# Weight buffers moved by 64 bytes, and thirteen products 32 columns wider, in a two-layer transformer step

## The chip, the cores and the metric

The kernel runs on one core of a Trainium2 chip. Its time is that of the whole program in device microseconds, the median of several runs. A profiled execution gives the trace from which all views here are taken.

Engines: TensorE (PE; its weight loads are listed as PEld), VectorE (DVE), ScalarE (ACT), GpSimd (POOL), SyncE (SP), and 16 DMA engines. SBUF is the on-chip memory of 128 partitions; an address below is a byte offset within a partition.

## What is computed

One step of a model with two layers, for 128 context tokens and 128 latent tokens, all in float32. Each layer is a mixer (attention) and a feed-forward; the change touches the feed-forward of the first layer alone:

```python
def conv_ffn(h, w_up, w_conv, b_conv, w_down):
    u = h @ w_up                                   # (128, 2048) x (2048, 11264), for both groups
    up = jnp.pad(u, ((0, 0), (1, 1), (0, 0)))
    u = up[:, :-2] * w_conv[0] + up[:, 1:-1] * w_conv[1] + up[:, 2:] * w_conv[2] + b_conv
    gate, val = u[..., :D_FF], u[..., D_FF:]       # D_FF = 5632
    return (jax.nn.silu(gate) * val) @ w_down
```

Around it stand a normalisation with a learned shift and scale before, and a gate and a residual sum behind it. The shifts, scales and gates come from a large product of the condition with `w_ada`.

## The kernel before

Both groups of tokens are kept together as 256 columns, features on the partitions. A product of float32 accuracy is made of three in the type float32r: each operand is split into a high and a low part, and `gemm` (line 382) issues, for each block of 128 features, high weights by high activations, high weights by low ones, and low weights by high ones. Each is one weight load of 128x128 and one product with 256 moved columns, all from the one line 111. A chunk is one output block of 128 features: 16 blocks, so 48 products, in the up-projection; 22 blocks, so 66 products, in the down-projection. The activations are `hx` (up) and `g` (down), high and low halves of 256 columns side by side in one row of 512.

The feed-forward (`ffn`, line 1527) goes in two halves: 44 up chunks (gate and value chunks in turn, each followed by the convolution `cv`), 16 down chunks, and the same again. So there are four parts: up, down, up, down.

Weights come through the class `Weights` (line 254). SP issues a DMA of 1 MB into `raw` (three buffers). The first 8 blocks are copied by ACT into `wh` (high part, line 249), and DVE subtracts to make `wl` (line 250), four buffers each, used in turn by the second 8 blocks too. In the first feed-forward two tiles in five take another way for their second 8 blocks (`go_far`, `prepare`, lines 287 to 302): ACT copies into `farh` (line 299), ACT writes its negative into `farl` (line 300), and POOL issues a DMA (line 301) that reads the weights from memory once more and adds them into `farl`, so that DVE needn't. There are two buffers of each, 43 far half-tiles of 24 products in all, 30 of them in up chunks. Nothing else in the program uses `farh` and `farl`.

Beside this, DVE works off the `w_ada` sums (line 499, tile `araw`) between its other work, at rates fixed by the table `FRATE`.

The tile framework fixes the order of instructions on each engine when the program is built, and places every buffer. The places that matter here, by the built program, in bytes:

| tile | role | first byte | remainder by 128 |
|---|---|---|---|
| `hx` | moved operand, up | 27,264 | 0 |
| `g` | moved operand, down | 151,168 (22 tiles, the others from 153,216 on) | 0 |
| `wh`, `wl` | weights | 104,128 and 120,512 (first of four each) | 64 |
| `farh`, `farl` | weights | 212,608 and 220,800 (first of two each) | 0 |

All blocks in these tiles are multiples of 512 bytes apart, so that the remainder is the same for all of them.

Products of more columns than needed are in the kernel already: the first products of five up chunks of each feed-forward move more than 256 columns (`WIDER`, 32, 16, 8, 4 and 2 more, through `more` in `gemm`). The surplus columns of the result are never read. In the second mixer, the list `PUSH` does the like.

Of the kernel before, what the change touches and what calls it, by code (L numbers as in the profile page):

```python
# [18 lines left out]
P = 128  # L19
# [3 lines left out]
NT = 2 * T  # L23
# [30 lines left out]
RATE = {"in0": 0.35, "in": 0.5, "in3": 0.25, "heads": 0.72, "out0": 0.62, "c": 0.36, "outc": 0.36}  # L54
FRATE = [{"up": 0.9, "down": 1.8}, {"up": 0.7, "down": 1.42}]
LEAD = (9, 3)
PEW = {"heads": 1.0, "out0": 1.0, "c": 1.0}
QUIET = [4, 3, 3]
LATE = 3
# [2 lines left out]
WIDER = (32, 16, 8, 4, 2)  # L62
# [33 lines left out]
def step_kernel(ctx: ExitStack, tc: tile.TileContext, A: dict):  # L96
# [36 lines left out]
    def banks(name):  # L133
        return tc.tile_pool(name=name, bufs=1, space=PSUM)
# [3 lines left out]
    def nm(s):  # L138
        uid[0] += 1
        return f"{s}_{uid[0]}"  # L140

    def T_(pl, shape, tag, dt=F32, bufs=None):
        kw = {} if bufs is None else {"bufs": bufs}
        return pl.tile(shape, dt, tag=tag, name=nm(tag), **kw)
# [11 lines left out]
    def C(name):  # L156
        a, w = _AT[name]
        return cst[:, a:a + w]
# [89 lines left out]
    def split(out_hi, out_lo, src, pin=lambda i: i):  # L248
        pin(act.copy(out_hi, src))  # L249
        pin(dve.tensor_tensor(out=out_lo, in0=src, in1=out_hi.bitcast(F32), op=ALU.subtract))  # L250

    fine = [False]

    class Weights:

# [35 lines left out]
        def prepare(self):  # L291
            while len(self.begun) < 2 and self.at < self.until:
                self.begun.append(self.load())
            for raw, n in self.begun:
                i = next(i for r, i in self.index if r is raw)
                if i in self.span and i % 5 in (1, 3) and not any(m[0] is raw for m in self.made):
                    wh = T_(self.far, [P, 1024], "farh", F32R, bufs=2)
                    wl = T_(self.far, [P, 1024], "farl", F32R, bufs=2)
                    act.copy(wh, raw[:, 8 * P:n * P])
                    act.activation(wl, wh.bitcast(F32), AF.Copy, scale=-1.0)  # L300
                    pool.dma_start(out=wl, in_=self.src[i, :, 8 * P:n * P], accum_op=ALU.add)
                    self.made.append((raw, wh, wl))
# [182 lines left out]
    def load_row():  # L485
        feat["row"] = T_(feat["home"], [P, 2, D], "condb")
        sp.dma_start(out=feat["row"], in_=A["condb"])
        for r in range(2):
            keep_order(act.activation(feat["row"][:, r], feat["row"][:, r], AF.Silu))
# [30 lines left out]
    class Deep:  # L520
# [44 lines left out]
        def pump(self):  # L565
            self.due += self.rate
            while self.due >= 1.0:
                self.due -= 1.0
                if self.steps:
                    self.step()  # L570
# [82 lines left out]
    def ensure(l, j, qs=range(4)):  # L653
        for u in [(l, j, q) for q in qs]:
            while u in ROWS and u not in done and ada["i"] <= ROWS.index(u):
                row_step()
            while u in FEATS and u not in done:
                feature_step()
            while u in DEEP[l] and u not in done:
                deep.step()  # L660
            while u not in done:
                later.pop(0)()
# [95 lines left out]
    def raw_tile(pl, tag):  # L758
        return home(pl, tag)[:, :KD * 2 * UW].rearrange("p (k n) -> p k n", k=KD)
# [183 lines left out]
    def mixer_ab(hx, beside):  # L943
        l = 0
        with tc.tile_pool(name="ab", bufs=1) as ab:
# [297 lines left out]
            with tc.tile_pool(name="abh", bufs=1) as hp:  # L1243
                ada["pew"] = PEW["heads"]

# [91 lines left out]
    def out_ab(o, st, u, beside, rp):  # L1337
        l = 0
        rows = raw_rows(u, l, 1)
        ensure(l, 2)  # L1340
        ada["pew"] = PEW["out0"]
        W = Weights(A["w_out_ab"], KD, 1)
# [184 lines left out]
    def ffn(hx, W, ready, turn, l, st):  # L1527
        xh, xl = (lambda k: hx[:, k, :NT]), (lambda k: hx[:, k, NT:2 * NT])
        wider = list(WIDER)
        long = len(ready) > 3  # L1530

        def product():
            if ready:
                return ready.pop(0)
            if in_order:
                return gemm(W.chunk(), xh, xl, between=in_order.pop(0))
            if wider:
                n = NT + wider.pop(0)
                return gemm(W.chunk(), xh, xl, more=lambda k: hx[:, k, :n])
            return gemm(W.chunk(), xh, xl)  # L1540

        WD = Weights(A["w_down"][l], KQ, TB)
        cw = ada["cw"]
        with tc.tile_pool(name=f"ffn{l}", bufs=1) as fp, banks(f"pffn{l}") as pf:
            feat["home"], feat["pool"] = fp, pf
            feat["due"] = 0.0
            in_order = [{}, {}] + turn + [{}]
            T_(fp, [P, SHIFT // 4], "pad")

            def conv(m):  # L1550
                early = bool(ready)
                pin = keep_order if early else lambda i: i
                if len(ready) > 4 - 2 * long:
                    W.ahead(pin)
                ps = product()
                y = T_(fp, [P, NT], "cv", bufs=3)
                pin(act.activation(y, ps, AF.Identity, scale=cw[:, 1, m:m + 1], bias=cw[:, 3, m:m + 1]))  # L1557
                y3 = y.rearrange("p (g t) -> p g t", g=2)
                p3 = ps.rearrange("p (g t) -> p g t", g=2)
                pin(dve.scalar_tensor_tensor(out=y3[:, :, 1:], in0=p3[:, :, :T - 1],  # L1560
                                             scalar=cw[:, 0, m:m + 1], in1=y3[:, :, 1:],
                                             op0=ALU.mult, op1=ALU.add))
                pin(dve.scalar_tensor_tensor(out=y3[:, :, :T - 1], in0=p3[:, :, 1:],  # L1563
                                             scalar=cw[:, 2, m:m + 1], in1=y3[:, :, :T - 1],
                                             op0=ALU.mult, op1=ALU.add))
                if early and ready and not long:
                    W.ahead(pin)
                return y

            def up(q):  # L1570
                gs = []
                for i in range(q * KQ, (q + 1) * KQ):
                    rate = 0 if i < LATE else FRATE[l]["up"]
                    fine[0] = False
                    gate = conv(i)
                    pump(0, rate)
                    val = conv(NFF + i)
                    pump(0, rate)
                    act.activation(gate, gate, AF.Silu)
                    dve.tensor_tensor(out=val, in0=gate, in1=val, op=ALU.mult)  # L1580
                    g = T_(fp, [P, ROW], "g", F32R, bufs=KQ)
                    split(g[:, :NT], g[:, NT:2 * NT], val)
                    gs.append(g)
                    if i == LATE - 1:
                        load_row()
                return gs

            def down(gs, q):
                u, rows = None, None
                if q == NQ - 1 and l < NL - 1:  # L1590
                    u = raw_tile(keep, "hx")
                    rows = raw_rows(u, l + 1, 0)
                for c in range(KD):
                    quiet = q == NQ - 1 and c >= KD - QUIET[0]
                    fine[0] = quiet
                    if q == 0:
                        ensure(l, 5, [c // 4])
                    ps = gemm(WD.chunk(), lambda k: gs[k][:, :NT], lambda k: gs[k][:, NT:2 * NT])
                    if l == NL - 1 and q == NQ - 1 and c == KD - 1:
                        last_residual(ps, l, 1, c, st)  # L1600
                    else:
                        residual(ps, l, 1, c, st if q == NQ - 1 else None)
                    if rows:
                        rows(c)
                    if l == NL - 1 and q == NQ - 1 and c in EARLY:
                        act.activation(x[:, c], x[:, c], AF.Identity, scale=C("gfin")[:, c:c + 1])
                    pump(0, 0 if quiet else FRATE[l]["down"])
                return u

            for q in range(NQ):  # L1610
                if l == 0:
                    at, n = 2 * KQ * q, KQ * KD // TB
                    W.go_far(fp, at + LEAD[q], at + 2 * KQ, at + 2 * KQ)
                    WD.go_far(fp, n * q + 3, n * q + n, n * q + n - 6 * q)
                gs = up(q)
                u = down(gs, q)
            while feat["i"] < FLIMIT[stage[0]]:
                feature_step()
            return u
# [26 lines left out]
    with tc.tile_pool(name="cc", bufs=1) as cp, banks("pc") as ppool["ada"]:  # L1646
# [6 lines left out]
        st = stat_init()  # L1653
        ada["pew"] = PEW["c"]
        u = mixer_c(cp, hx, W, begun[0], st)
# [155 lines left out]
```

## Time and profile before

| what | value |
|---|---|
| median of 3 runs | 2322.39 us (2319.88 to 2324.16) |
| profiled execution | 2326.57 us, span 2324.8 us |
| mean granted TensorE clock | 0.993 |
| first feed-forward, first chunk with a wider product to last down product | 481.07 to 1193.22 us |
| second feed-forward, the same | 1632.28 to some 2312 us |
| DMA | 639.68 MB, mean 275 GB/s |

The page gives busy shares by engine and the chain of work that ended last. The windows view counts instructions in stretches of the span: since TensorE never rests, a stretch's length divided by its count of products is the time from one product to the next. The timeline lists instructions with their starts; equal neighbours are merged into one row with a count, and brackets tell what an engine waited for.

### The profile page before, as it was taken

To read this page: it belongs to the slowest core of one execution; us is meant where nothing else is said; L and a number is where in the kernel's file an instruction comes from. 1 tells how busy PE (TensorE), PEld (TensorE's weight loads), DVE (VectorE), ACT (ScalarE), POOL (GpSimd) and SP (SyncE) were. 2 spreads that over 40 slices of the span, in tenths; PEclk is the share of its full clock that TensorE was granted. 3 is DMA by queue.
4 is the path that set the end of the run, shared out by engine and by line. 5 is a ranking of instruction groups with operands and counts; after the bars stand their busy time and mean duration, and the time that the engine had idled before them with its cause. 6 is when DMAs were issued, how large, how long until landed. Compare 5 with 4: busy or idle time off the path is not lost.

```text
span 2324.8 us, 47335 instructions
## 1 busy us (share of the span) xinstructions
PE 2292.3 (99%) x19388; PEld 2209.0 (95%) x19388; DVE 1888.9 (81%) x2975; ACT 1231.6 (53%) x1999; POOL 227.8 (10%) x281
## 2 busy tenths in 40 slices
PE   8899999999999999999999999999999999999998
PEld 6788878999999999999999999999999999999998
DVE  4668979889888998989978989998999965666654
ACT  4346555675554455555565455557655434555543
POOL 0012111300000000000230000024000000000011
PEclk9999999999999999999999999999999999999999
DMA  9988879789889999998977887766767655555553
GB/s 380 366 335 307 327 287 366 290 296 305 293 301 318 350 318 305 304 311 291 325 262 268 338 277 272 257 217 214 253 259 269 257 200 198 188 195 200 188 194 127
DMA packets 106313, 639.68 MB, mean 275 GB/s; under 512 B 11440, under 2 KB 19568, under 8 KB 39536
## 3 DMA queue, kind: packets, MB, share of 16 engines
q1 hardware_dynamic: 99904, 614.11, 71.1%
q0 software_dynamic: 6192, 22.55, 5.3%
q8 instruction: 152, 2.49, 0.4%
q14 instruction: 65, 0.53, 0.1%
HBM read 631.86 MB, written 4.75 MB: 274 GB/s over the span
## 4 chain that ended last, share of the span: by engine, by line
PE 94%; DVE 2%; DMA 2%; POOL 1%; ACT 1%; issue 0%; SPq 0%; DVEq 0%; ACTq 0%; POOLq 0%
PE acc L111 89%; PE ada L111 3%; PE att L111 2%; DMA kvb<-w_ada 1%; DVE wl L250 1%; PE att L114 1%; DMA farl<-w_up 0%; PE misc L111 0%; DMA araw<-w_ada 0%; POOL dev L833 0%; DVE hx L551 0%; PE ada L114 0%; DVE x L1668 0%; POOL hxc L837 0%; ACT wh L249 0%
## 5 line engine op out<-in xcount | busy, mean ns | idle before, releaser
L111 PE MATMUL acc<-hx,wh 128*128 128x256 f32 (+1 forms) x6784 | 1188.8, 280 | 5.2 <-ACT wh L249 1.7
L249 ACT CAST wh<-raw 128x1024 fp32r<-128x1024 f32 (+2 forms) x791 | 749.7, 961 | 765.7 <-PE acc L111 637.4
L250 DVE TENSOR_TENSOR wl<-raw,wh 128x1024 fp32r<-128x1024 f32 (+2 forms) x791 | 876.3, 1121 | 264.6 <-ACT wh L249 260.8
L111 PEld LDWEIGHTS acc<-hx,wh 128*128 128x128 f32 x6784 | 1032.8, 189 | 24.0 <-issue 8.5
L111 PE MATMUL acc<-hx,wl 128*128 128x256 f32 (+1 forms) x3392 | 946.0, 279 | 4.7 <-DVE wl L250 4.4
L111 PEld LDWEIGHTS acc<-hx,wl 128*128 128x128 f32 x3392 | 639.5, 189 | 8.1 <-DVE wl L250 6.3
L111 PE MATMUL acc<-g,wh 128*128 128x256 f32 x2608 | 452.7, 279 | 0.0
L111 PEld LDWEIGHTS acc<-g,wh 128*128 128x128 f32 x2608 | 396.6, 189 | 0.0
L111 PE MATMUL acc<-g,wl 128*128 128x256 f32 x1304 | 362.5, 278 | 0.0
L499 DVE CUSTOM_DVE_ANT_0 junk<-araw,condb 128x2048 f32<-128x2048 f32 x152 | 349.5, 2299 | 1.3 <-DMA araw<-w_ada 1.3
L111 PEld LDWEIGHTS acc<-g,wl 128*128 128x128 f32 x1304 | 245.1, 188 | 0.0
L111 PE MATMUL acc<-hxc,wh 128*128 128x256 f32 (+1 forms) x1056 | 188.9, 281 | 0.0
L111 PEld LDWEIGHTS acc<-hxc,wh 128*128 128x128 f32 x1056 | 161.7, 188 | 1.0 <-issue 0.8
L212 POOL TENSOR_TENSOR sqacc<-sqacc,sq 128x256 f32<-128x256 f32 x62 | 73.1, 1178 | 878.6 <-ACT sq L208 878.4
L111 PE MATMUL acc<-hxc,wl 128*128 128x256 f32 (+1 forms) x528 | 146.8, 278 | 0.0
L1557 ACT ACTIVATE cv<-acc,convw 128x256 f32<-128x256 f32 x169 | 94.3, 558 | 19.9 <-PE acc L111 19.7
L111 PEld LDWEIGHTS acc<-hxc,wl 128*128 128x128 f32 x528 | 99.5, 189 | 0.2
L111 PE MATMUL acc<-wh,hxc 128*128 128x256 f32 (+1 forms) x512 | 94.3, 282 | 0.8 <-DVE nt L844 0.8
L111 PE MATMUL acc<-hx,farh 128*128 128x256 f32 x480 | 88.6, 285 | 0.0
L551 DVE CUSTOM_DVE_ANT_0 hx<-block,condb 128x1024 fp32r<-128x1024 f32 x65 | 79.4, 1222 | 6.8 <-DMA block<-w_ada 6.3
L1563 DVE SCALAR_TENSOR_TENSOR cv<-acc,convw,cv 128x254 f32<-128x254 f32 x169 | 81.1, 480 | 3.5
L1560 DVE SCALAR_TENSOR_TENSOR cv<-acc,convw,cv 128x254 f32<-128x254 f32 x169 | 80.5, 477 | 3.3 <-ACT cv L1557 3.3
(275 smaller groups left out, 2280.3 us busy)
## 6 DMA issues: line engine op xcount, KB each, us to landing
raw<-w_up SPq DMA_DIRECT2D x176, 1024.0 KB, 5.3
araw<-w_ada SPq DMA_DIRECT2D x136, 1024.0 KB, 6.9
raw<-w_down SPq DMA_DIRECT2D x88, 1024.0 KB, 5.0
raw<-w_in_c SPq DMA_DIRECT2D x48, 1024.0 KB, 6.6
block<-w_ada SPq DMA_DIRECT2D x41, 512.0 KB, 5.9
raw<-w_in_ab SPq DMA_DIRECT2D x18, 1024.0 KB, 9.2
raw<-w_out_ab SPq DMA_DIRECT2D x16, 1024.0 KB, 8.1
raw<-w_out_c SPq DMA_DIRECT2D x16, 1024.0 KB, 6.1
```

The costliest lines, as they stand in the source:

```text
L111: return self.placed(nc.tensor.matmul(*a, **kw))
L114: return self.placed(nc.tensor.transpose(*a, **kw))
L212: eng.tensor_tensor(out=st["acc"], in0=st["acc"], in1=sq, op=ALU.add)
L249: pin(act.copy(out_hi, src))
L250: pin(dve.tensor_tensor(out=out_lo, in0=src, in1=out_hi.bitcast(F32), op=ALU.subtract))
L499: keep_order(dve.tensor_tensor_reduce(out=T_(feat["pool"], [P, D], "junk"), in1=feat["row"][:, c], in0=feat["raw"].rearrange("p g n -> p ( ...
L551: keep_order(dve.tensor_tensor_reduce(out=self.junk, in0=self.raw, in1=self.row[:, c].rearrange("p (g n) -> p g n", g=2), scale=1.0, scala ...
L1557: pin(act.activation(y, ps, AF.Identity, scale=cw[:, 1, m:m + 1], bias=cw[:, 3, m:m + 1]))
L1560: pin(dve.scalar_tensor_tensor(out=y3[:, :, 1:], in0=p3[:, :, :T - 1], scalar=cw[:, 0, m:m + 1], in1=y3[:, :, 1:], op0=ALU.mult, op1=ALU.add))
L1563: pin(dve.scalar_tensor_tensor(out=y3[:, :, :T - 1], in0=p3[:, :, 1:], scalar=cw[:, 2, m:m + 1], in1=y3[:, :, :T - 1], op0=ALU.mult, op1=A ...
```

## The change

A pad of 16 floats (64 bytes) is allocated once, ahead of the first `farh`. It moves `farh` to 212,672 and `farl` to 220,864, so that both have the remainder 64 by 128. No other tile of the program moves. And in the first feed-forward (`l == 0`), of the up chunks counted from the first one that has a wider product, each sixth one gets a first product that moves 288 columns instead of 256. The first of those, chunk 6, comes after the five of `WIDER`.

```diff
+FARPAD = 16
+BEAT = 6
...
     fine = [False]
+    pads = []
...
                 if i in self.span and i % 5 in (1, 3) and not any(m[0] is raw for m in self.made):
+                    if not pads:
+                        pads.append(T_(self.far, [P, FARPAD], "farpad"))
                     wh = T_(self.far, [P, 1024], "farh", F32R, bufs=2)
                     wl = T_(self.far, [P, 1024], "farl", F32R, bufs=2)
...
         wider = list(WIDER)
+        ups = [0]
...
-            if wider:
-                n = NT + wider.pop(0)
+            ups[0] += 1
+            if wider or l == 0 and ups[0] % BEAT == 0:
+                n = NT + (wider.pop(0) if wider else WIDER[0])
                 return gemm(W.chunk(), xh, xl, more=lambda k: hx[:, k, :n])
```

In the built program, DVE, ACT, POOL and SP have the same instructions in the same order as before, and so has TensorE but for 13 products' width: 6 in the first up part, 7 in the second. The line numbers behind the edits shift (111 becomes 113).

On TensorE, at the end of the first chunk that has far weights and the start of the next one, in the first up part, stood before (each row is output tile <- moved operand, weights; numbers tell buffers apart):

```order
L111 MATMUL acc_6107<-hx_5342,farh_5956 128x256 x2
L111 MATMUL acc_6107<-hx_5342,farl_5957 128x256
L111 MATMUL acc_6179<-hx_5342,wh_6171 128x256 x2
L111 MATMUL acc_6179<-hx_5342,wl_6172 128x256
L111 MATMUL acc_6179<-hx_5342,wh_6171 128x256 x2
```

In the same place stands now:

```order
L113 MATMUL acc_6108<-hx_5342,farh_5957 128x256 x2
L113 MATMUL acc_6108<-hx_5342,farl_5958 128x256
L113 MATMUL acc_6180<-hx_5342,wh_6172 128x288
L113 MATMUL acc_6180<-hx_5342,wh_6172 128x256
L113 MATMUL acc_6180<-hx_5342,wl_6173 128x256
L113 MATMUL acc_6180<-hx_5342,wh_6172 128x256 x2
```

Nothing moved: the first product of the chunk behind the far half-tile has 288 columns, which parts the merged row in two.

The second place is again on TensorE: the fifth chunk of the second up part, the first wide product behind the first down part. Before:

```order
L111 MATMUL acc_10006<-hx_5342,wh_10002 128x256 x2
L111 MATMUL acc_10006<-hx_5342,wl_10003 128x256
L111 MATMUL acc_10072<-hx_5342,wh_10068 128x256 x2
L111 MATMUL acc_10072<-hx_5342,wl_10069 128x256
L111 MATMUL acc_10072<-hx_5342,wh_10068 128x256 x2
```

And now:

```order
L113 MATMUL acc_10007<-hx_5342,wh_10003 128x256 x2
L113 MATMUL acc_10007<-hx_5342,wl_10004 128x256
L113 MATMUL acc_10073<-hx_5342,wh_10069 128x288
L113 MATMUL acc_10073<-hx_5342,wh_10069 128x256
L113 MATMUL acc_10073<-hx_5342,wl_10070 128x256
L113 MATMUL acc_10073<-hx_5342,wh_10069 128x256 x2
```

Between the last wide product of the first up part and this one lie the rest of that part, the whole first down part and four up chunks, all with weights from `wh`, `wl` and the moved `farh`, `farl`.

## The prediction

> **What bounds the kernel now.** I read the page's busy shares first, then the chain that ended last.
>
> ```profile
> PE 2292.3 (99%) x19388; PEld 2209.0 (95%) x19388; DVE 1888.9 (81%) x2975; ACT 1231.6 (53%) x1999; POOL 227.8 (10%) x281
> ...
> PE acc L111 89%; PE ada L111 3%; PE att L111 2%; DMA kvb<-w_ada 1%; DVE wl L250 1%; PE att L114 1%; DMA farl<-w_up 0%; PE misc L111 0%; DMA araw<-w_ada 0%; POOL dev L833 0%; DVE hx L551 0%; PE ada L114 0%; DVE x L1668 0%; POOL hxc L837 0%; ACT wh L249 0%
> ```
>
> TensorE is busy for 99% of the span, and 89% of the chain are the products of line 111. An always busy engine gets faster only by doing each product faster, so the next view is the pace of the products: the windows view, cut at the ends of the four parts of the first feed-forward (up, down, up, down), and for comparison a long piece of the second one. Columns: window and length, then busy time (and count) of PE, its weight loads, DVE, ACT and POOL, granted clock, DMA share, GB/s. (A window also counts the product or two under way at its start.)
>
> ```profile
> 505.69:693.66 187.97, 185.78 (x1563) 185.55 (x1562) 165.34 (x216) 104.03 (x142) 10.37 (x12) 0.99 0.90 302
> 693.66:818.98 125.32, 125.32 (x1057) 125.32 (x1057) 112.68 (x133) 54.28 (x54) 6.90 (x8) 1.00 0.95 332
> 818.98:1068.58 249.60, 249.60 (x2114) 249.60 (x2113) 225.32 (x289) 139.03 (x189) 13.86 (x16) 1.00 0.90 306
> 1068.58:1193.22 124.64, 124.64 (x1058) 124.64 (x1057) 112.99 (x162) 67.02 (x113) 21.28 (x19) 1.00 0.84 293
> 1660.00:2300.00 640.00, 640.00 (x5649) 640.00 (x5649) 460.48 (x601) 316.97 (x418) 15.38 (x13) 1.00 0.60 214
> ```
>
> Length by count: the second feed-forward takes 640/5649 = 113.3 ns a product, the first 124.64/1058 = 117.8 ns and more. Same shape (128x128 weights, 256 columns), same engine, same granted clock of 1.00, PE busy throughout. So there are two paces, **113.3 and 117.8 ns**, and each holds for hundreds of microseconds. The question is what moves TensorE from one to the other. The timeline of PE shows where the good pace ends (columns: start, length of the merged row, operation, count):
>
> ```profile
> 505.35 0.39 PE L111 MATMUL acc<-hx,wh 128*128 128x256 f32 x2
> 505.57 0.28 PE L111 MATMUL acc<-hx,wl 128*128 128x256 f32 x1
> 505.69 0.40 PE L111 MATMUL acc<-hx,farh 128*128 128x256 f32 x2
> 505.93 0.28 PE L111 MATMUL acc<-hx,farl 128*128 128x256 f32 x1
> 506.05 0.40 PE L111 MATMUL acc<-hx,farh 128*128 128x256 f32 x2
> ```
> ```profile
> 508.56 0.40 PE L111 MATMUL acc<-hx,wh 128*128 128x256 f32 x2
> 508.80 0.28 PE L111 MATMUL acc<-hx,wl 128*128 128x256 f32 x1
> ```
>
> Three products take 505.69 - 505.35 = 0.34 us up to the first weights out of farh and farl, then 506.05 - 505.69 = 0.36 us: 113 becomes 120 ns with exactly that product. Behind the far half-chunk, weights from wh and wl again, it is 508.80 - 508.56 = 0.24 us for two: the pace doesn't come back, though nothing waits. By the program's places, the moved operand hx (and g) starts at a multiple of 128 bytes, the weights in wh and wl 64 bytes past one, those in farh and farl at a multiple. So far weights are the only ones that share the moved operand's remainder, and they have a pace of their own (120 ns).
>
> **The change, part by part.**
>
> *The buffers 64 bytes on.* No instruction is added or removed on any engine and no row changes its place; farh and farl get the remainder that wh and wl have. If the remainder is the cause, far weights no longer throw TensorE out of the good pace, which then holds as in the second feed-forward. The products of the four parts after 505.69 are, by the code, 32.5 and 44 up chunks of 48 and twice 16 down chunks of 66: 5,784. They took 187.97 + 125.32 + 249.60 + 124.64 = 687.5 us; at 113.3 ns they take 655.3. Of these 32.2 us some aren't pace:
>
> ```profile
> 687.37 0.40 PE L111 MATMUL acc<-hx,farh 128*128 128x256 f32 x2
> 689.95 0.38 PE L111 MATMUL acc<-hx,farl 128*128 128x256 f32 x1 [2.19 <-DMA farl<-w_up]
> ...
> 692.38 0.63 PE L111 MATMUL acc<-hx,farh 128*128 128x256 f32 x2
> 692.80 0.41 PE L111 MATMUL acc<-hx,farl 128*128 128x256 f32 x1
> ```
> ```profile
> 690.00:695.00 5.00, 5.00 (x29) 5.00 (x30) 5.00 (x8) 0.98 (x2) 0.00 (x0) 0.66 0.95 369
> ```
>
> Two products fill 687.37 to 689.95: 2.58 - 0.23 = 2.35 us of waiting for a far transfer. Then products stand 0.21 us apart (692.38 to 692.80) at a granted clock of 0.66 over these 5 us; a third of 5 us lost is 1.7. Together 4 us that an address doesn't cure. **Term 1: -28.2 us.** From below it is bounded by the far products alone: 43 tiles of 24 products, (120 - 117.8) ns each, 2.3 us.
>
> *The wider products.* The rows of the order show 13 of them, each on an up chunk's first product. What one costs at the good pace, and what one does at the bad pace, the trace has already (first rows: first feed-forward; second: the second one):
>
> ```profile
> 481.07 0.41 PE L111 MATMUL acc<-hx,wh 128*128 128x288 f32 x2
> ...
> 481.80 0.39 PE L111 MATMUL acc<-hx,wh 128*128 128x256 f32 x2
> 482.03 0.28 PE L111 MATMUL acc<-hx,wl 128*128 128x256 f32 x1
> ```
> ```profile
> 1631.93 0.40 PE L111 MATMUL acc<-hx,wh 128*128 128x256 f32 x2
> 1632.16 0.28 PE L111 MATMUL acc<-hx,wl 128*128 128x256 f32 x1
> 1632.28 0.41 PE L111 MATMUL acc<-hx,wh 128*128 128x288 f32 x2
> ...
> 1633.00 0.39 PE L111 MATMUL acc<-hx,wh 128*128 128x256 f32 x2
> 1633.22 0.28 PE L111 MATMUL acc<-hx,wl 128*128 128x256 f32 x1
> ```
>
> Six products from 481.07 to 481.80 take 0.73 us instead of 0.68, and then two take 0.23 again: 0.05 us, and the good pace returns. **Term 2: 13 x 0.05 = +0.65 us.** At 1632 it is 0.35 us for three before and 0.22 for two soon after: the wide product took TensorE from 117.8 to 113.3. It doesn't always:
>
> ```profile
> 1295.21 0.48 PE L111 MATMUL acc<-hxc,wh 128*128 128x288 f32 x1
> 1295.53 0.28 PE L111 MATMUL acc<-hxc,wl 128*128 128x256 f32 x1
> 1295.64 0.40 PE L111 MATMUL acc<-hxc,wh 128*128 128x256 f32 x2
> 1295.88 0.28 PE L111 MATMUL acc<-hxc,wl 128*128 128x256 f32 x1
> ```
>
> Here, behind attention, two still take 0.24 us. So the 13 are a repair with a chance, not a certainty, and they stand in the up parts only.
>
> *What is late next.* Suppliers must keep up with a TensorE 4% faster. Over 505 to 1195:
>
> ```profile
> 505.00:1195.00 690.00, 687.81 (x5807) 687.58 (x5806) 618.60 (x803) 366.14 (x503) 52.41 (x55) 1.00 0.90 307
> ```
> ```profile
> ACT wh L249 <- PE acc L111: 161.3, 102, 4.3
> ```
> ```profile
> 511.00:514.00 3.00, 3.00 (x28) 3.00 (x27) 2.26 (x5) 1.05 (x1) 0.00 (x0) 1.00 1.05 384
> ```
>
> DVE has 618.6 us of work and would have 662: 93%. ACT waits 161 us for TensorE to give back weight buffers, so casts run ahead. DMA moves 307 GB/s, would need 320, and reached 384. None becomes the bound on average. The far transfers are the thin place:
>
> ```profile
> 678.73 0.86 POOL L301 DMA_DIRECT2D farl<-w_up  x1 [12.90 <-ACT farl L300]
> ```
> ```profile
> DMA to landing us min/median/max: 5.3/8.4/12.1
> ```
>
> Issue at 678.73, wanted some 8.9 us later (687.6), landed at 689.95. A 4% faster TensorE wants such a tile 0.4 us earlier, and behind the waiting product stands all of TensorE, in order. Between nothing (all but the slowest land in time) and 43 x 0.4 = 17 us (each is late by what it lost) I take a sixth of the tiles, since the median lies 3.7 us under the slowest: **Term 3: +3 us**. A stall may also end the good pace. Between nothing and all of the first down part (1,056 products x 4.5 ns = 4.8 us, no wide product in it) I take half: **Term 4: +2.4 us**.
>
> Sum: -28.2 + 0.65 + 3 + 2.4 = **-22.2 us**. The profiled execution took 2326.57 (span 2324.8), 4.2 above the median of the three runs, so it gives 2304.4 by the profile and **2300 by the median**, 2322.39 - 22.2.
>
> **A rule against it.** Far products take 120 ns where wh products take 117.8 or 113.3, all at full clock. The Trainium skill, TensorE: Matmul & The Clock Gate, section Step-by-step: what each phase is for, says that TensorE has two independent SBUF read ports, so that "Loading the next tile's weights doesn't steal SBUF read bandwidth from the running matmul". By that rule the weights' address is indifferent and the first rival holds and the sum is its -2 us instead of -22; the rows just named speak against it, without showing that the remainder is what matters.
>
> **The rivals.**
>
> 1. *The address isn't the cause* (another trait of the far tiles is, say that a DMA adds into them). Far half-chunks keep breaking the pace. Each wide product then buys at best the chunks up to the next far one, about one of 48 products x 4.5 ns = 0.2 us: 13 x 0.2 - 0.65 = -2 us, 2320. For it: no other weights lie at a multiple of 128, so the trace can't separate the two. Against: the far pace sets in within one product, and the places fit. 8%.
> 2. *Relapse.* The pace holds until a late far tile, as at 687, breaks it, and repairs often fail as at 1295. Gain in the first up part alone, 1,560 x 4.5 ns = 7.0 us, and two thirds of the second, 6.3: with term 2 -12.7, 2310; with the first part alone 2316. 22%.
> 3. *Slower: late far tiles pile up.* Place: farl in the first feed-forward. A stall like 687's costs 2.35 us, and 1.7 more by the lower clock: 4 us. The gain of 27.6 is used up by seven; from nine on the kernel is slower by over 0.2%. Twelve give +20, 2343. For it: transfers with median 8.4 and maximum 12.1 us, against 8.9 from issue to use above. Against: at 117.8 ns it happened once, and a stall lets the transfers catch up. 10%. The Trainium skill, same page, section Why this matters for your kernels, warns of gaps over some 3 us; the trace's clock fell after 2.35.
>
> **How the numbers follow.** My forecast, the pace held through most of the first feed-forward, has 60% and by itself 2292 (-28.2 + 0.65 and most of the stall gone too) to 2308 (term 3 at 10 us). The range takes in rival 2 and ends at 2316. Rivals 1 and 3 stay outside, 18%. Faster by over 0.2% (about what a measurement of this kernel can tell from no change): 60 + 22 = 82%; within it: 8%; slower: 10%.
>
> **What would show it.** The windows of the four parts should count one PE product per 113.3 ns, far half-chunks too, and the timeline at 505.7 no step. 120 ns on far weights would prove rival 1. 113.3 up to a wait on a far transfer and 117.8 behind it is rival 2. More waits for farl and a clock under 1 in several windows is rival 3. The forecast is wrong if far weights at the new place run at 117.8 with no return to 113.3.

## The result, and the profile after

| kernel | median of the runs | lowest to highest | profiled execution (span) |
|---|---|---|---|
| before | 2322.91 us, 4 runs | 2319.88 to 2324.16 | 2326.57 (2324.8) |
| after | 2310.59 us, 4 runs | 2308.41 to 2312.83 | 2309.2 (2307.4) |

The ratio is 0.9949, 95% interval 0.9932 to 0.9966: faster by 12.3 us, where 22.2 were forecast. The two profiled executions lie further apart, 17.4 us, because the one of before was 3.7 above its median and the one of after 1.4 below. What follows is read from these two, so it adds up to 17.4.

The page of after, busy shares and the chain that ended last:

```profile
PE 2266.9 (98%) x19388; PEld 2182.6 (95%) x19388; DVE 1888.2 (82%) x2975; ACT 1228.8 (53%) x1999; POOL 229.4 (10%) x281
...
PE 81%; DMA 7%; DVE 5%; issue 4%; ACT 1%; POOL 1%; SPq 0%; DVEq 0%; ACTq 0%; POOLq 0%
```

TensorE has as many instructions as before and is busy 25.4 us less. In the chain it no longer stands alone: transfers have 7%, where the page of before has 2%. So the products got faster, and something else now ends last in places. The windows view, cut as before at the first far product and the ends of the four parts (columns: window and length, then busy time and count of PE, PEld, DVE, ACT, POOL, granted clock, DMA share, GB/s):

```profile
507.33:691.87 184.54, 179.56 (x1563) 178.75 (x1562) 164.99 (x216) 103.15 (x142) 10.37 (x12) 0.99 0.91 307
691.87:811.80 119.93, 119.93 (x1057) 119.93 (x1057) 112.10 (x133) 54.27 (x54) 6.90 (x8) 1.00 0.98 346
811.80:1054.26 242.46, 241.19 (x2114) 240.82 (x2113) 221.79 (x286) 138.12 (x188) 13.86 (x16) 1.00 0.92 311
1054.26:1178.73 124.47, 122.87 (x1058) 122.24 (x1057) 117.09 (x167) 66.97 (x114) 24.86 (x19) 1.00 0.89 306
```

The same 5,784 products take 671.4 us instead of 687.5: 16.1 of the 17.4. The first down part has no idle time: 119.93 / 1057 = 113.5 ns a product, where it was 125.32 / 1057 = 118.6 before. The others miss that pace by different amounts, and the first, third and fourth have idle time (184.54 - 179.56 = 5 us in the first). At the place where before stepped from 113 to 120 ns, the timeline of after shows no step:

```profile
506.99 0.39 PE L113 MATMUL acc<-hx,wh 128*128 128x256 f32 x2
507.22 0.28 PE L113 MATMUL acc<-hx,wl 128*128 128x256 f32 x1
507.33 0.39 PE L113 MATMUL acc<-hx,farh 128*128 128x256 f32 x2
507.56 0.28 PE L113 MATMUL acc<-hx,farl 128*128 128x256 f32 x1
507.67 0.39 PE L113 MATMUL acc<-hx,farh 128*128 128x256 f32 x2
```

Three products take 0.34 us on both sides of the first far weights. What holds TensorE now is in the waits view of after, PE, over these parts (total us, times, longest):

```profile
PE acc L113 <- DMA farl<-w_up: 5.1, 4, 2.4
PE acc L113 <- DMA farl<-w_down: 1.3, 1, 1.3
PE acc L113 <- DVE wl L252: 0.7, 1, 0.7
PE acc L113 <- DVE cv L1570: 0.5, 1, 0.5
```

In before this view has one row of a far tile, the 2.2 us that the prediction quoted. The longest one of after, in the timeline:

```profile
685.13 0.39 PE L113 MATMUL acc<-hx,farh 128*128 128x256 f32 x2
687.90 0.39 PE L113 MATMUL acc<-hx,farl 128*128 128x256 f32 x1 [2.38 <-DMA farl<-w_up]
...
689.30 0.64 PE L113 MATMUL acc<-hx,farh 128*128 128x256 f32 x2
689.73 0.41 PE L113 MATMUL acc<-hx,farl 128*128 128x256 f32 x1
689.95 0.63 PE L113 MATMUL acc<-hx,farh 128*128 128x256 f32 x2
```

Two products fill 2.77 us, and a microsecond later three take 0.65 us instead of 0.34, until just past the end of the part.

To compare the kernels, the starts of these 5,784 products in each trace were added up in three heaps, each over 113.33 ns a product (0.34 us for three): products that start over 0.26 us after the one before ("waits", with their number), those 0.15 to 0.26 us behind it ("half clock": 16 of the 28 of after run at half the granted clock, as at 689, and most of the others come right behind a wait), and the rest ("pace").

| profiled execution | waits | half clock | pace | sum |
|---|---|---|---|---|
| before | 2.4 (1) | 1.8 | 27.9 | 32.0 |
| after | 9.3 (9) | 2.7 | 3.9 | 15.9 |

So 24 us of pace were won, and 7.8 us of them went into waits and into the slow products behind them. Of the 9.3 us of waits, 7.5 are for six far tiles; the other three waits are for work of DVE and ACT (`wl`, `cv`, `g`).

### The profile page after: what moved, and what is told of

Read it like the earlier page. It is cut to its first block, busy times and chain, and to the rows that moved or that the text cites. A ratio compares the mean times of both kernels' runs of the same rounds, so it can differ in the third digit from the quotient of the medians.

```text
span 2307.4 us, 47336 instructions
## 1 busy us (share of the span) xinstructions
PE 2266.9 (98%) x19388; PEld 2182.6 (95%) x19388; DVE 1888.2 (82%) x2975; ACT 1228.8 (53%) x1999; POOL 229.4 (10%) x281
## 4 chain that ended last, share of the span: by engine, by line
PE 81%; DMA 7%; DVE 5%; issue 4%; ACT 1%; POOL 1%; SPq 0%; DVEq 0%; ACTq 0%; POOLq 0%
PE acc L113 76%; DMA raw<-w_up 2%; PE ada L113 2%; DVE wl L252 2%; PE att L113 2%; DMA farl<-w_up 1%; DMA raw<-w_down 1%; DVE junk L504 1%; DMA kvb<-w_ada 1%; DMA raw<-w_in_ab 1%; ACT wh L251 1%; PE att L116 1%; DVE hx L556 0%; DMA farl<-w_down 0%; POOL dev L838 0%
## 5 line engine op out<-in xcount | busy, mean ns | idle before, releaser
L113 PE MATMUL acc<-hx,wh 128*128 128x256 f32 (+1 forms) x6784 | 1175.6, 278 | 5.5 <-ACT wh L251 1.7
L113 PE MATMUL acc<-g,wh 128*128 128x256 f32 x2608 | 446.9, 277 | 0.1
L304 ACT CAST farh<-raw 128x1024 fp32r<-128x1024 f32 x43 | 45.3, 1053 | 86.5 <-DMA raw<-w_up 59.5
L1570 DVE SCALAR_TENSOR_TENSOR cv<-acc,convw,cv 128x254 f32<-128x254 f32 x169 | 80.9, 479 | 3.5
```

Source lines behind the costliest of these rows:

```text
L113: return self.placed(nc.tensor.matmul(*a, **kw))
```

## The experiments

Times are medians; "sum" and its parts are those of the table above, in us, from the experiment's profiled execution. Ratios are against the kernel before, timed beside each experiment (medians 2320.93 to 2323.03 us); the changed kernel's own is 0.9949 (0.9932 to 0.9966). Diffs are against the changed kernel unless said otherwise.

### The two parts of the change alone

The place without the wider products:

```diff
-            if wider or l == 0 and ups[0] % BEAT == 0:
+            if wider:
```

> The buffers 64 bytes on, without the 13 wider products. If the place of the far buffers is what counts (theory A): far half-chunks keep 113.3 ns, the first up and down parts run as in the changed kernel, but whatever a late transfer breaks stays broken until another wait mends it, so 2310 to 2316 us. If the wider products do the work (theory K): 2320 us or more, far half-chunks throw the pace to 117.8 ns at 507 us and it stays there.

Measured: 2314.94 us, 12 runs from 2306.57 to 2322.75, ratio 0.9970 (0.9956 to 0.9983). Its profiled execution was one of the long ones, 2321.67, and shows how runs can come to differ so much. The good pace holds, with interruptions, up to this place in the timeline:

```profile
656.71 0.39 PE L113 MATMUL acc<-hx,wh 128*128 128x256 f32 x2
656.94 0.28 PE L113 MATMUL acc<-hx,wl 128*128 128x256 f32 x1
657.05 0.39 PE L113 MATMUL acc<-hx,farh 128*128 128x256 f32 x2
660.69 0.40 PE L113 MATMUL acc<-hx,farl 128*128 128x256 f32 x1 [3.25 <-DMA farl<-w_up]
```

and this is its windows view from there on:

```profile
700.00:1180.00 480.00, 479.77 (x4074) 479.56 (x4073) 438.79 (x562) 252.09 (x342) 40.85 (x42) 1.00 0.92 314
```

480 / 4074 = 117.8 ns: one wait put TensorE into the slower pace, and with no wider product it stayed there to the end of the feed-forward (pace 21.0, sum 29.6). How far the good pace lasted in the other eleven runs no trace tells.

The wider products without the place (the pad's two lines left out):

> The 13 wider products with the far buffers at their old place. Theory A: each far half-chunk runs at 120 ns and leaves 117.8 behind it; a wide product brings 113.3 back only up to the next far half-chunk, at most some 0.2 us each: 2320 to 2322 us. Theory K: about the 2310.6 us of the changed kernel.

Measured: 2319.24 us, 11 runs from 2317.21 to 2322.61, ratio 0.9991 (0.9983 to 1.0000). Pace 24.7, sum 27.0. In its trace each of the 13 wider products brings the pace back, from 118 or 120 ns to 113, and the next far weights end it again. One of them:

```profile
678.89 0.40 PE L113 MATMUL acc<-hx,farh 128*128 128x256 f32 x2
679.13 0.28 PE L113 MATMUL acc<-hx,farl 128*128 128x256 f32 x1
679.24 0.42 PE L113 MATMUL acc<-hx,wh 128*128 128x288 f32 x2
...
679.97 0.39 PE L113 MATMUL acc<-hx,wh 128*128 128x256 f32 x2
680.19 0.28 PE L113 MATMUL acc<-hx,wl 128*128 128x256 f32 x1
680.31 0.39 PE L113 MATMUL acc<-hx,wh 128*128 128x256 f32 x2
```

679.24 - 678.89 = 0.35 us for three before, 680.31 - 679.97 = 0.34 behind it. The place gives the pace; the wider products win it back, and alone are worth some 2 us, which the interval hardly tells from nothing.

### Which places are good

Four kernels move the buffers by another distance and change nothing else (`FARPAD` 32, 64, 8 and 48 floats: 128, 256, 32 and 192 bytes).

> The pad 128 bytes instead of 64: the far buffers move as well, but their remainder by 128 is 0 again, as before. Theory A (the remainder): no gain but that of the wider products, 2319 to 2322 us, far products at 120 ns. Rival (any other place, or the distance to some other buffer): as the changed kernel, 2310 us, far products at 113.3 ns.

> The pad 256 bytes: remainder by 256 as in the kernel before (128, that of hx and g), by 512 another. If the remainder by 256 decides (theory A256): far products at a steady 120 ns and 117.8 ns behind them as in the run of wide products alone, 2317 to 2321 us. If a longer period or another distance decides: far products as with a pad of 128 bytes (uneven, 118 ns in the mean, 113.3 behind them) or of 64 (113.3).

> The pad 32 bytes: remainder 32 by 128. If a difference of remainders of at least 64 is needed: far products above 113.3 ns, between the 118 and 120 of the pads 128 and 0, 2313 to 2320 us. If any difference is enough: 113.3 ns, about 2310 us.

> The far buffers go 192 bytes on, so that their first bytes leave a remainder of 64 by 256; hx and g leave 128, wh and wl 192. Theory A: what counts is that weights and moved operand lie 64 bytes apart within 256, on either side. Then far products take 113.3 ns as in the changed kernel, and the time is the changed kernel's, 2306 to 2314. Theory B: only the remainder that wh and wl have (192) is good, and any other one costs, as 32 and 128 bytes on did (about 118 ns in the far half-chunks, 113.3 behind them): 1032 far products by some 4.5 ns more, 2311 to 2317. Theory C: no rule by remainders; then the far pace may be 120 ns as with 0 and 256 bytes, with 117.8 behind it: 2317 to 2325. The far products' own pace in the trace tells the three apart better than the time.

Measured, with before and after for comparison. `hx` and `g` leave 128 by 256 in all of them, `wh` and `wl` 192. The median is that over the far products' distances from start to start, without waits and half clock.

| bytes on | remainder by 256 | from `hx`, `g` | far products, median | pace | sum | time |
|---|---|---|---|---|---|---|
| 0, before | 128 | 0 | 120 ns | 27.9 | 32.0 | 2322.91 |
| 32 | 160 | 32 | 117 ns | 7.2 | 21.7 | 2313.67, one run |
| 64, after | 192 | 64 | 113 ns | 3.9 | 15.9 | 2310.59 |
| 128 | 0 | 128 | 119 ns | 6.9 | 23.8 | 2313.70 (2308.67 to 2317.78, 5 runs), ratio 0.9968 (0.9956 to 0.9979) |
| 192 | 64 | 64 | 113 ns | 3.4 | 22.9 | 2308.50 (2302.73 to 2316.72, 5 runs), ratio 0.9937 (0.9915 to 0.9959) |
| 256 | 128 | 0 | 120 ns | 23.9 | 30.4 | 2324.62, one run |

The view of the tile `farl` shows the same in the products' durations (min/median/max in ns, first and last start). With 256 bytes:

```profile
L113 PE MATMUL acc<-hx,farl x240: 281/283/582, 507.9 to 1063.2; 128*128 128x256 f32 x120
```

and with 192:

```profile
L113 PE MATMUL acc<-hx,farl x240: 276/276/417, 505.9 to 1054.9; 128*128 128x256 f32 x120
```

The prediction's remainder by 128 is refuted by the kernel with 128 bytes: by 128 it stands where before does, yet TensorE comes back to 113.3 ns right behind the far half-tiles, without a wider product:

```profile
547.08 0.40 PE L113 MATMUL acc<-hx,farh 128*128 128x256 f32 x2
547.31 0.28 PE L113 MATMUL acc<-hx,farl 128*128 128x256 f32 x1
547.43 0.40 PE L113 MATMUL acc<-hx,wh 128*128 128x256 f32 x2
547.67 0.28 PE L113 MATMUL acc<-hx,wl 128*128 128x256 f32 x1
547.79 0.39 PE L113 MATMUL acc<-hx,wh 128*128 128x256 f32 x2
...
548.13 0.39 PE L113 MATMUL acc<-hx,wh 128*128 128x256 f32 x2
```

548.13 - 547.79 = 0.34 us for three. By 256 the rows of the table are in order. The same remainder as the moved operand gives 120 ns and a slow pace that stays; 64 bytes apart, on either side, costs nothing; 32 and 128 apart cost some 4 to 5 ns on the far products themselves and leave the pace behind them alone. The kernel with 192 bytes also rules out that `farh` and `farl` have to match `wh` and `wl`. Its time can't be told from that of after: its profiled execution, at 2314.47, had 16.5 us of waits.

In all these kernels only the weights moved. By themselves they can't tell a distance to the moved operand from places that are bad for weights whatever moves. The second mixer can. There the roles are exchanged: the weights come from `hxc`, which by the built program of before starts at byte 148,096, remainder 128 by 256 like the far weights of before, and the moved operand is `wh` or `wl`, remainder 192. In the trace of before, 72 such products in a row run at the good pace from 1259.27 us on:

```profile
1259.50 0.39 PE L111 MATMUL acc<-wh,hxc 128*128 128x256 f32 x2
1259.73 0.28 PE L111 MATMUL acc<-wl,hxc 128*128 128x256 f32 x1
1259.84 0.39 PE L111 MATMUL acc<-wh,hxc 128*128 128x256 f32 x2
```

Three take 0.34 us. Of the eight stretches of this kind two run like this and the others at 117.8 ns, none at 120. So the remainder 128 isn't bad for weights as such, and the distance to the moved operand is what counts.

### Where the rest of the gain went

Half the load of the `w_ada` sums. This kernel leaves out every second `w_ada` transfer of the sums that DVE works off, so that they use old data:

```diff
-        if c == 0:
+        if c == 0 and t % 2 == 0:
```

> The changed kernel with every second transfer of w_ada for VectorE's sums left out (it sums the tile before twice; that part of the result is not computed). If late far transfers come from transfers that compete (theory C), the waits for farl, some 8 us in the changed kernel, go to under 2 us, and with them most relapses: 2298 to 2303 us. If they come from late issue by POOL and ACT alone, the waits stay and the time stays within 3 us of 2310.6.

Measured: 2308.22 us, 6 runs from 2305.22 to 2316.44, ratio 0.9952 (0.9938 to 0.9967). Both views of the tile `farl` give the time from issue to landing; first after, then this kernel:

```profile
DMA to landing us min/median/max: 5.3/8.2/11.2
```
```profile
DMA to landing us min/median/max: 5.1/6.1/10.9
```

The transfers landed 2.1 us earlier in the median, and two far tiles instead of six were waited for. But these two, the first of them here,

```profile
685.84 0.58 PE L113 MATMUL acc<-hx,farl 128*128 128x256 f32 x1 [2.79 <-DMA farl<-w_up]
686.22 0.63 PE L113 MATMUL acc<-hx,farh 128*128 128x256 f32 x2
686.64 0.41 PE L113 MATMUL acc<-hx,farl 128*128 128x256 f32 x1
```

cost 5.7 us, and some 40 products at half clock behind them: waits 7.4, half clock 4.6, together the 12.0 of after. In this execution less load made a late tile rarer, and the two slowest transfers cost as much as the six of after.

More wider products, each third chunk of up and down parts:

```diff
-BEAT = 6
+BEAT = 3
...
+                    wide = (lambda k: gs[k][:, :NT + WIDER[0]]) if l == 0 and c % 3 == 2 else None
+                    ps = gemm(WD.chunk(), lambda k: gs[k][:, :NT], lambda k: gs[k][:, NT:2 * NT], more=wide)
```

> The changed kernel with a wider first product on each third up chunk instead of each sixth, and on each third down chunk of the first feed-forward too. If relapses behind waits cost what the trace of the changed kernel shows (117.8 ns from 854 to 868 us, 1015 to 1026 us, 1120 to 1178 us: 3.2 us; theory A with repair), these go to under 1 us and 22 more wide products cost 1.1: about 2309 us by the median and a narrower spread of runs. If a wide product breaks the pace as often as it mends it, 117.8 ns fills more of the parts: 2311 to 2316 us.

Measured: 2313.92 us, 5 runs from 2309.22 to 2314.36, ratio 0.9963 (0.9950 to 0.9977). Pace 2.8 instead of 3.9, waits and half clock 18.5. The relapses were small already, so there was little to repair. The time lies in the range of the second expectation, but not for its reason: the pace got no worse, and the waits were longer. Whether the edit made them longer, or one execution differs from another by as much, one trace can't say.

Four of the far tiles that had been late made by DVE instead:

```diff
+NOT_FAR = (38, 41, 43, 51)
...
-                if i in self.span and i % 5 in (1, 3) and not any(m[0] is raw for m in self.made):
+                if i in self.span and i % 5 in (1, 3) and not (self.per == 1 and i in NOT_FAR) and not any(m[0] is raw for m in self.made):
```

> The changed kernel with four of the 30 far half-tiles of the up parts made by VectorE instead (tiles 38, 41, 43 and 51, those TensorE waited for at 656, 673, 685 and 853 us). If the waits for late far transfers are what the change lost (theory C'): 5.7 us of waits and 1.6 us of half clock at 689 us go, 4 x 1.2 us more for VectorE stay hidden: 2302 to 2305 us. If the waits only move to the next tile or to VectorE: 2309 to 2312 us.

Measured: 2312.04 us, 5 runs from 2309.11 to 2317.22, ratio 0.9962 (0.9949 to 0.9976). Its waits over the same parts:

```profile
PE acc L114 <- DMA farl<-w_up: 4.0, 2, 2.5
PE acc L114 <- DMA farl<-w_down: 3.6, 3, 2.1
PE acc L114 <- DVE wl L253: 2.3, 3, 1.0
```

The first up part lost its waits for far tiles (it is 2.1 us over the good pace, where after is 7.7); others came later, at 705, 839, 979, 1097 and 1126 us. Its pace heap is 7.2, for there were more relapses. Which tile is late isn't a trait of the tile.

No far transfers. The low part of the far weights is left as the negative high part, without the weights added into it:

```diff
-                    pool.dma_start(out=wl, in_=self.src[i, :, 8 * P:n * P], accum_op=ALU.add)
```

> The changed kernel without the transfers into farl (farl keeps the negative of the high part, so the low part of the far weights is wrong); all products, casts and sums stay. If the late far transfers are where the rest of the expected gain went (theory C'): no wait for farl, hardly a relapse, 113.3 ns nearly throughout, some 11 us less than the changed kernel: 2296 to 2302 us. If casts, sums or weight transfers would be late in their stead: waits of TensorE for wh or wl of 5 us or more, 2305 to 2310 us.

Measured: 2294.28 us, 4 runs from 2292.69 to 2294.90, ratio 0.9877 (0.9862 to 0.9892). Its windows, cut at the same products:

```profile
507.99:685.07 177.08, 177.08 (x1562) 177.08 (x1561) 165.19 (x216) 105.17 (x142) 0.00 (x0) 1.00 0.77 282
685.07:804.75 119.68, 119.68 (x1058) 119.68 (x1057) 113.31 (x133) 54.10 (x54) 0.00 (x0) 1.00 0.84 311
804.75:1044.44 239.69, 239.69 (x2115) 239.69 (x2113) 223.87 (x289) 140.71 (x189) 0.00 (x0) 1.00 0.76 284
1044.44:1164.12 119.68, 119.68 (x1059) 119.68 (x1057) 113.04 (x162) 66.43 (x113) 21.55 (x14) 1.00 0.77 284
```

TensorE is busy for the whole of each window, 656.1 us for all four: 0.6 over the good pace, which is 13 wider products by 0.05. The other 15.3 us of after are gone, and the time falls by 16.3. So the far transfers are what stands between after and the good pace throughout. Whether by landing late or by their load on the DMA engines this kernel can't say, since both go. The kernel with half the sums kept the transfers and took load away (over the first up part its DMA share is 0.83, that of after 0.91, that without transfers 0.77); it kept the 12.0 us, which speaks against the load alone without settling it. Here DVE works 165.19 of 177.08 us and keeps up, and the few waits for `wl` are gone too.

The same edit in the kernel before (old place, no wider products):

> The kernel before without the transfers into farl (far weights' low part wrong in the same way), the buffers at their old place. If the place sets the pace (theory A): far products at 120 ns and 117.8 ns behind them as ever, 2316 to 2321 us. If the transfers that add into the buffers do (the first rival of the forecast): 113.3 ns through the far half-chunks, 2300 us or less.

Measured: 2320.4 us, one run. From its windows and its view of `farl`:

```profile
690.09:814.88 124.79, 124.79 (x1058) 124.79 (x1057) 114.43 (x135) 54.17 (x54) 0.00 (x0) 1.00 0.79 299
```
```profile
L111 PE MATMUL acc<-hx,farl x240: 281/283/283, 505.9 to 1058.7; 128*128 128x256 f32 x120
```

117.9 ns a product and 283 ns for far ones, as before, at a granted clock of 1.00 and a DMA share of 0.79, with no wait at all (pace 28.0). The slow pace is neither the work of a transfer that adds into the weights nor of the load on the DMA engines: at the new place the pace is good at nearly the same DMA share, 0.77.

The sums spread thinner over the first feed-forward:

```diff
-FRATE = [{"up": 0.9, "down": 1.8}, {"up": 0.7, "down": 1.42}]
+FRATE = [{"up": 0.83, "down": 1.66}, {"up": 0.7, "down": 1.42}]
```

> The changed kernel with VectorE's sums of w_ada spread over more of the first feed-forward (rates 0.83 and 1.66 instead of 0.9 and 1.8 per chunk; the same sums and transfers, 8% thinner; the last one still ends before the last down chunks). If thinner competing transfers and work make the far transfers land in time (theory C): 2304 to 2308 us. If the waits only move: 2309 to 2313 us.

Measured: 2337.03 us, 5 runs from 2334.34 to 2341.84, ratio 1.0066 (1.0053 to 1.0079). Both expectations missed, because neither looked at what is left over. Its waits view, PE, whole span:

```profile
PE att L113 <- DVE mod L504: 14.8, 1, 14.8
```

What the feed-forward doesn't work off, the attention of the second layer needs at once; TensorE stood for 14.8 us at 1192 to 1207 us, a wait that after doesn't have. Of the rest, 12.9 us are in the feed-forward itself, more waiting above all (waits 20.2, half clock 4.1, pace 4.5; far tiles of up parts 9.0 us, `wl` 4.9).

Whether the edit made these waits or they are the scatter of one execution stays open: the kernel with 192 bytes waited nearly as long at the rates of after.

No kernel here that computes everything is faster than after beyond the runs' spread.

## Why the prediction was right, and what was mis-sized

The forecast held in direction, mechanism and range; it promised 22.2 us and the profiles give 17.4, the medians 12.3. By its terms:

1. *Term 1, the pace (-28.2).* Right. The pace heap of before is 27.9, and without transfers (above) all of it goes. The cause was named rightly as the place of the far weights against the moved operand, and wrongly as a remainder by 128: it is one by 256. A pad of 64 bytes, taken over from `wh` and `wl`, is right by either rule; that the wrong one did no harm was luck.
2. *Term 2, the wider products (+0.65).* Right: 0.6 for 13 in the kernel without transfers.
3. *Term 3, late far transfers (+3).* **This step failed, in size.** It measured +7.8: waits and half clock went from 4.2 to 12.0. Waits for far tiles are 5.2 of it (2.35 to 7.5), waits for DVE and ACT 1.7, slow products 0.9. The step said that "a 4% faster TensorE wants such a tile 0.4 us earlier", and took a sixth of the tiles. The number of tiles was right: 6 of 43 were waited for. The 0.4 us was wrong. From the issue of its transfer to the moment when TensorE wanted it, the one late tile of before had 8.9 us and the others 10.8 to 16.2, median 13.7; those of after had 7.8 to 16.6, median 11.7, and thirteen of them less than 10.8. The lead fell by 2.0 us by the medians (1.6 in the median from tile to tile), not by the 4% of one chunk, while the transfers took as long as ever (median 8.4 us from issue to landing before, 8.2 after). So a late tile cost 1.3 us on average (7.5 us for six, over the good pace), up to 2.5, and the longest wait brought slow products with it. That the lead shrinks because the loads ahead of a far tile come no faster, so that a faster TensorE eats up their head start chunk by chunk, would fit; no run isolates it.
4. *Term 4, relapse after a wait (+2.4).* About right: 3.3, the pace heap of 3.9 less the wider products. Three relapses: after the far wait at 853 us, a delay of some 0.05 us at 1015, at a product whose `wl` DVE had only just finished, and the far wait at 1118. The first one ended as the row at 1632 of before had it, at a wider product (868 us), the second one at the wait for `cv` (1026 us).

The one in the last down part, where no wider product stands, lasted to the end, at 58.00 / 495 = 117.2 ns and more (a window counts a product or two under way at its start):

```profile
1120.30:1178.30 58.00, 58.00 (x495) 58.00 (x494) 53.25 (x82) 30.70 (x58) 12.49 (x9) 1.00 0.81 286
```

The sum by measured terms: -27.9 + 0.6 + 7.8 + 3.3 = -16.2 us; the remaining 1.2 of the profiles' 17.4 lie outside these parts. From the profiles to the medians it is the 3.7 + 1.4 us of the first section: the forecast took the difference that it read from one profiled execution for that of the medians.

*The rivals.* Rival 1 (the adding transfer is the cause) fell by the kernels with and without transfers at both places. What stood for it, that no other weights lie at a multiple of 128, wasn't so: those of `hxc` in the second mixer do, and the trace of before had them at the good pace. Its time for a repair alone, 2320, is close to the 2319.24 of the wider products without the place. The rule of the Trainium skill, TensorE: Matmul & The Clock Gate, section Step-by-step: what each phase is for, that weight loads take no read bandwidth from a running product, was taken to mean that the weights' address is indifferent, which gave 2320 for the change. These runs contradict that consequence: at equal clock and without a wait, one place of the weights costs 120 ns and another 113.3. Whether read bandwidth is what the place costs, no run here shows. Rival 2 (relapse for good) is what one execution of the kernel without wider products did; in after two of three relapses were short. Rival 3 (late tiles pile up until it is slower) was right in its mechanism, six far tiles waited for instead of one, and wrong in the price: its 4 us a tile belongs to the longest one alone, the others cost 0.3 to 1.5 us, and six aren't nine.

## What to carry to other kernels

When TensorE never waits, divide windows by their counts: equal work at 113 and 118 ns at the same granted clock is a loss that no busy share shows, and the timeline tells which operand begins it. Compare the byte offsets of weights and moved operand by 256, and try 64 apart (measured here for float32r, with 128x128 weights and 256 moved columns alone). And when a bound engine gets 4% faster, measure the lead of each transfer it waits for, issue to first use, against landing: the lead can shrink by much more than 4% of one step, and only the kernel without the transfers shows how much of the gain is still to be had.

## What the runs showed that was not expected

- The place acts by 256 bytes and in three grades: 120 ns a far product and a lasting 117.8 behind it (same remainder), 117 to 119 in the far products alone (32 and 128 apart), 113 (64 apart on either side). Why the first alone lasts is open.
- A wait can set off the slow pace, even a delay of some 0.05 us, but most waits don't, and one (1026 in after) ended it. A product of 288 columns brought the good pace back 13 times of 13 with the buffers at the old place; behind attention, at 1295 of before, it didn't.
- The granted clock fell to 0.50 behind the wait of 2.4 us at 685 in after (sixteen products) and behind one of 2.8 us with half the sums (26 products). The length of a wait alone doesn't decide it: behind one of 3.1 us, at 978 in the kernel with 192 bytes, the clock stayed at 1.00, and so it did behind one of 2.5 us, at 979 in the kernel with four far tiles less. The windows behind the wait in after and behind that of 3.1 us:

```profile
689.00:692.00 3.00, 3.00 (x16) 3.00 (x16) 3.00 (x6) 0.42 (x1) 0.00 (x0) 0.50 1.00 360
```
```profile
981.60:986.60 5.00, 5.00 (x43) 5.00 (x44) 5.00 (x9) 3.72 (x5) 0.88 (x1) 1.00 0.94 324
```

The Trainium skill, TensorE: Matmul & The Clock Gate, section Why this matters for your kernels, warns of gaps over some 3 us; here 2.4 us were enough in one place, and 3.1 us weren't in another.

- The first packet of a far transfer of 512 KB comes 1.6 to 4.8 us after its issue. The six of after that were waited for all started more than 3.1 us behind it and landed 9.2 to 11.2 us after it. What holds the first packet back is open.
